# Weight parts moved to other byte offsets inside their tiles

## The chip, the cores and the metric

The kernel runs on one core of one Trainium2 chip. The metric is the device time in microseconds (us); for one core it is the time of that core. Times are medians of several executions; the profile is one further execution.

## The reference, cut to what matters

A decoder of two layers, for 512 tokens of width 1024, in float32. Layer 0 mixes tokens with a gated delta rule (6 heads, run in chunks), layer 1 with sliding-window attention (12 query heads that share two heads of keys and values); both also attend to 256 memory tokens. Each layer ends in a SwiGLU feed-forward of width 2816.

```python
for layer in range(DEPTH):
    h = rms_norm(x, ln_mix[layer])
    mkv = mem_n @ w_mem_kv[layer]
    ...
    x = x + jnp.concatenate([mix_out, mem_o], axis=-1) @ w_out[layer]
    x = x + swiglu(rms_norm(x, ln_ffn[layer]), w_gate_up[layer], w_down[layer])
return rms_norm(x, ln_final)
```

The change touches no product; it concerns where the weights of these products lie in on-chip memory while TensorE reads them.

## The kernel before, in words

**Three products for one.** Every float32 operand of a large product is split into a high part, rounded to the type float32r, and a low part, the remainder. `split` does that with two instructions: ScalarE copies the source to the high part (line 148, by way of `copy`) and VectorE subtracts the high part from the source (line 161, by way of `tt`). `mm3` then issues three matmuls for each 128 rows of the contraction: high weight with high activation, high weight with low activation, low weight with high activation. In the profile the weight tiles are called `whi` and `wlo`, and all these matmuls stand on line 154.

**Two operands, two streams.** In each matmul the weight block of 128x128 floats is the stationary operand: LDWEIGHTS reads 128 floats (512 bytes) from each partition. The activation is the moving operand: 512 floats (2048 bytes) or 256 floats (1024 bytes) are read from each partition while the matmul runs. The load for the next matmul runs beside the present matmul. The profile shows matmuls as engine PE and weight loads as engine PEld.

**Two kinds of weights.** `weight` loads a whole row of weights ([128, 1024], sometimes 768 or fewer columns) from memory, takes a pair of tiles from `parts()` and splits into them. These are the wide weights. They serve `project` (input projections, gates of the feed-forward, queries, output projection), the down projections and the memory keys and values; the moving operand there is nearly always 512 wide. The other kind is narrow. In the feed-forward, two columns of the gate or up matrix are computed at a time by a scheme with seven products of half size in place of eight (`quarters`). Each product takes a weight part of 512 columns and moving operands 256 wide. Those parts lie in a ring of six places: `ring()` takes three pairs of tiles from `parts()` and puts two halves in each pair, and `product` takes the places in turn. A product is four calls of `mm3`, so 12 matmuls; a call of `quarters` has seven products.

**Where the tiles begin.** A weight tile from `parts()` has 1024 + SPARE floats, with SPARE = 64; that is 4352 bytes, 17 times 256. The activation tiles have 2048 bytes and the token sums (tag `T`) 4096. As the program places them, all of these begin at the same place modulo 256 bytes. Every step inside a tile is a multiple of 256 bytes too: 512 bytes from one weight block to the next, 1024 from one half of the tokens to the other, 2048 from one ring half to the other. So the distance modulo 256 between a matmul's moving operand and its weight block is given by the offset inside the weight tile alone. This text calls the distance (moving address minus weight address, modulo 256) the lag. The ring halves begin SHIFT = 16 floats, 64 bytes, into their tile, so their lag is 192. The wide weights begin at offset 0, so their lag is 0. The last down projection takes its weights from another pool (`own`, tag `T`), also with lag 0.

**Order of the work.** Each engine's queue is filled in program order. The stages are: memory keys and values; the delta-rule layer; its output projection; its feed-forward; the attention layer; its output projection; its feed-forward. A feed-forward handles 12 and then 10 of the 22 column pairs; each part is a stretch of ring products followed by a stretch of down projections.

Of the kernel before, what the change touches and what calls it, by code (L numbers as in the profile page):

```python
# [19 lines left out]
T = 512  # L20
# [7 lines left out]
FT = DFF // P  # L28
EPS = 1e-6
LINE = 64  # L30
SHIFT, SPARE = 16, 64
NEG = -1e30
BASE = 32
NB = P // BASE
# [54 lines left out]
class Builder:  # L89
    def __init__(self, tc, a):  # L90
        self.tc, self.nc, self.a = tc, tc.nc, a
        self.n = 0
        self.table, self.table_ins, self.table_users = None, None, []


    def t(self, pool, shape, dtype=F32, tag=None, bufs=None, name=None):
# [96 lines left out]
    def weight(self, src, eng=None, raw=None, parts=1, pool=None, tags=("whi", "wlo"), bufs=3):  # L193

        raw = self.load(src) if raw is None else raw
        n = raw.shape[1]
        if pool is None:
            hi, lo = (x[:, :n] for x in self.parts())
        else:
            hi, lo = (self.t(pool, [P, D], F32R, t, bufs)[:, :n] for t in tags)  # L200
        for i in range(parts):
            s = slice(i * n // parts, (i + 1) * n // parts)
            self.split(raw[:, s], hi[:, s], lo[:, s], eng or self.weng)
        return hi, lo
# [636 lines left out]
    def ffn(self, fp, xp, layer, h, apool, rope=False):  # L841
# [3 lines left out]
        acts, sums, open_pairs, places = [], [], [], []  # L845
# [18 lines left out]
        def ring():  # L864

            if not places:
                for _ in range(3):
                    two = self.parts()
                    places.extend(tuple(x[:, SHIFT + i * T:SHIFT + (i + 1) * T] for x in two) for i in range(2))
            places.append(places.pop(0))  # L870
            return places[-1]

        def begin(f, up, by, tag, bufs, then):

            o = [self.t(fp, [P, T], F32, tag, bufs) for _ in range(2)]
            steps = self.quarters(fp, [col(f + i, up) for i in range(2)], sums, by, o, ring)
            next(steps)
            end()
            next(steps)
            open_pairs.append((steps, then, o))  # L880
            return o
# [13 lines left out]
        for f0, half in ((0, 12), (12, 10)):  # L895
# [16 lines left out]
            for m in range(tail):  # L912
                ps = self.bank("pj")
                for j in (0, 6):
                    n = min(6, half - j)
# [8 lines left out]
        if tail < KD:  # L924
# [9 lines left out]
            for t in parts:  # L934
                acc = self.acc[:, t]
                for m in range(tail, KD):
# [3 lines left out]
                    x = self.x[m][:, t]  # L940
# [295 lines left out]
```

## Time and profile before

| | us |
|---|---|
| Median of 3 runs | 1162.48 (1160.89 to 1162.56) |
| The profiled execution, its own time | 1162.59 |
| Its span, first to last instruction | 1160.8 |
| PE busy | 1135.7 |
| PEld busy | 995.0 |
| DVE (VectorE) busy | 843.1 |
| ACT (ScalarE) busy | 635.5 |

The profiled execution spent 1.79 us outside its span and is 0.11 us above the median, so differences read from the span can be laid on the median as they are. The mean granted TensorE clock is 0.998 of full speed. A matmul's duration in the profile is longer than the time it holds up the next one, since matmuls are pipelined; the pace of a stretch of matmuls is its length divided by their number.

### The profile page before, as it was taken

The numbers are of one execution on the slowest core, as the hardware profiler recorded it, in microseconds if no ns is written. First come the engines' busy times: TensorE is split into PE (matmuls) and PEld (weight loads), VectorE is DVE, ScalarE is ACT, GpSimd is POOL, SyncE is SP. The second block draws the span as 40 slices with busy tenths as digits, with TensorE's granted clock in tenths as the row PEclk, the third lists the DMA queues.
The fourth block names the chain that finished last, engine by engine and source line by source line (L and its number), as shares of the span: only waits on it lengthen the run. The fifth ranks groups of instructions, "written<-read, shape, count | busy, mean of one in ns | idle before, by whom it ended". The sixth has DMA issues, their size and how long they took to land.

```text
span 1160.8 us, 19674 instructions
## 1 busy us (share of the span) xinstructions
PE 1135.7 (98%) x7476; PEld 995.0 (86%) x7476; DVE 843.1 (73%) x1587; ACT 635.5 (55%) x1273; POOL 85.8 (7%) x97
## 2 busy tenths in 40 slices
PE   7999999999999999999999999999999999999996
PEld 6878777877899998899998777677899988999986
DVE  5754877767789987489866767758799843798754
ACT  7569563366556652256653547675566622566533
POOL 0210000000111100011100000010011100111000
PEclk9999999999999999999999999999999999999999
DMA  8433352225567744567723421143477743577232
GB/s 308 129 108 114 115 127 92 73 91 164 163 141 186 188 124 129 151 149 188 173 75 98 136 73 38 55 99 120 113 186 191 175 111 104 150 188 179 74 93 94
DMA packets 73971, 152.83 MB, mean 132 GB/s; under 512 B 17756, under 2 KB 18420, under 8 KB 73876
## 3 DMA queue, kind: packets, MB, share of 16 engines
q1 hardware_dynamic: 62356, 130.59, 35.9%
q0 software_dynamic: 11520, 20.98, 11.5%
q8 instruction: 59, 0.97, 0.4%
q14 instruction: 36, 0.29, 0.1%
HBM read 144.58 MB, written 6.96 MB: 131 GB/s over the span
## 4 chain that ended last, share of the span: by engine, by line
PE 86%; DVE 8%; ACT 2%; DMA 2%; issue 1%; SPq 0%; DVEq 0%; ACTq 0%
PE pj L154 40%; PE g L154 38%; PE sc L154 6%; DVE wlo L161 2%; PE pt L158 1%; DMA wraw<-in_wout 1%; PE g L158 1%; ACT sm L142 1%; DVE l L164 1%; ACT whi L148 1%; DMA wraw<-in_wmk 1%; DVE btmp L161 1%; DVE big L161 0%; DVE sm L752 0%; PE qk L154 0%
## 5 line engine op out<-in xcount | busy, mean ns | idle before, releaser
L148 ACT ACTIVATE whi<-wraw 128x512 fp32r<-128x512 f32 (+2 forms) x331 | 244.2, 745 | 271.9 <-PE pj L154 175.2
L161 DVE TENSOR_TENSOR wlo<-wraw,whi 128x512 fp32r<-128x512 f32 (+2 forms) x331 | 274.3, 838 | 108.6 <-ACT whi L148 102.7
L154 PE MATMUL pj<-h,whi 128*128 128x512 f32 (+1 forms) x676 | 266.4, 395 | 0.8 <-ACT h L148 0.5
L154 PE MATMUL pj<-l,whi 128*128 128x512 f32 (+1 forms) x676 | 265.2, 392 | 1.2 <-DVE l L164 1.2
L154 PE MATMUL pj<-h,wlo 128*128 128x512 f32 (+1 forms) x676 | 265.3, 393 | 0.0
L154 PE MATMUL g<-T,whi 128*128 128x256 f32 x1280 | 230.3, 282 | 0.0
L154 PEld LDWEIGHTS g<-T,whi 128*128 128x128 f32 x1280 | 197.6, 190 | 1.6 <-DVE fu L164 1.6
L154 PE MATMUL g<-T,wlo 128*128 128x256 f32 x640 | 180.1, 281 | 0.0
L154 PEld LDWEIGHTS pj<-h,whi 128*128 128x128 f32 x676 | 127.1, 188 | 29.7 <-issue 3.0
L154 PEld LDWEIGHTS pj<-l,whi 128*128 128x128 f32 x676 | 127.2, 188 | 28.4 <-DVE l L164 2.0
L154 PEld LDWEIGHTS pj<-h,wlo 128*128 128x128 f32 x676 | 127.3, 188 | 26.3 <-issue 1.9
L154 PE MATMUL g<-h,wlo 128*128 128x256 f32 (+1 forms) x508 | 146.2, 288 | 0.0
L154 PE MATMUL g<-l,whi 128*128 128x256 f32 (+1 forms) x508 | 146.1, 288 | 0.0
L154 PE MATMUL g<-h,whi 128*128 128x256 f32 (+1 forms) x508 | 146.0, 287 | 0.0
L154 PEld LDWEIGHTS g<-T,wlo 128*128 128x128 f32 x640 | 120.2, 188 | 0.0
L154 PEld LDWEIGHTS g<-l,whi 128*128 128x128 f32 x508 | 97.5, 192 | 1.2
L154 PEld LDWEIGHTS g<-h,whi 128*128 128x128 f32 x508 | 95.4, 188 | 1.2
L154 PEld LDWEIGHTS g<-h,wlo 128*128 128x128 f32 x508 | 95.4, 188 | 1.2 <-issue 0.2
L985 POOL DMA_DIRECT2D ws<-in_wgu x40 | 35.2, 879 | 722.9 <-ACT sq L151 246.2
L148 ACT ACTIVATE whi<-ws 128x512 fp32r<-128x512 f32 x80 | 50.4, 631 | 51.2 <-PE g L154 42.0
L161 DVE TENSOR_TENSOR fu<-pj,rstd 128x512 f32<-128x512 f32 (+1 forms) x34 | 22.4, 659 | 54.8 <-PE pj L154 54.8
L161 DVE TENSOR_TENSOR wlo<-ws,whi 128x512 fp32r<-128x512 f32 x80 | 54.8, 685 | 6.9 <-ACT whi L148 6.8
(345 smaller groups left out, 1633.0 us busy)
## 6 DMA issues: line engine op xcount, KB each, us to landing
wraw<-in_wgu SPq DMA_DIRECT2D x48, 512.0 KB, 4.1
ws<-in_wgu SPq DMA_DIRECT2D x80, 256.0 KB, 3.5
ws<-in_wgu POOLq DMA_DIRECT2D x80, 256.0 KB, 4.8
wraw<-in_wdn SPq DMA_DIRECT2D x48, 384.0 KB, 3.2
wraw<-in_win SPq DMA_DIRECT2D x26, 512.0 KB, 3.7
wraw<-in_wgu SPq DMA_DIRECT2D x40, 256.0 KB, 4.4
wraw<-in_wout SPq DMA_DIRECT2D x16, 512.0 KB, 3.6
wraw<-in_wdn SPq DMA_DIRECT2D x16, 256.0 KB, 2.7
```

The costliest lines, as they stand in the source:

```text
L142: ins = self.nc.scalar.activation(out, in_, func, **kw).ins
L148: self.copied = self.nc.scalar.activation(out, in_, AF.Copy, **kw).ins
L154: return self.nc.tensor.matmul(out, lhsT, rhs, start=start, stop=stop, skip_group_check=more).ins
L158: return self.nc.tensor.transpose(out, in_, self.ident[:k, :k]).ins
L161: return eng.tensor_tensor(out=out, in0=a, in1=b, op=op).ins
L164: self.nc.vector.scalar_tensor_tensor(out=out, in0=in0, scalar=scalar, in1=in1, op0=op0, op1=op1)
L985: nc.gpsimd.dma_start(s1, a22, accum_op=ALU.add)
```

## The change

The single constant SHIFT goes. Each of the six ring halves gets its own offset, and the wide weights go through four offsets in turn, one step for each call of `weight` without a pool. The tile size stays, since SPARE stays at 64. High and low part of one weight always have the same offset. The numbers of instructions, transfers and waits do not change.

```diff
-SHIFT, SPARE = 16, 64
+NARROW, WIDE, SPARE = ((12, 20), (28, 52), (17, 60)), (4, 8, 60, 62), 64
...
+        self.wide = 0
...
         if pool is None:
-            hi, lo = (x[:, :n] for x in self.parts())
+            o = WIDE[self.wide % len(WIDE)]
+            self.wide += 1
+            hi, lo = (x[:, o:o + n] for x in self.parts())
...
-                for _ in range(3):
+                for shifts in NARROW:
                     two = self.parts()
-                    places.extend(tuple(x[:, SHIFT + i * T:SHIFT + (i + 1) * T] for x in two) for i in range(2))
+                    places.extend(tuple(x[:, o + i * T:o + (i + 1) * T] for x in two) for i, o in enumerate(shifts))
```

In bytes, the ring offsets 12, 20, 28, 52, 17 and 60 are 48, 80, 112, 208, 68 and 240; the lags are 208, 176, 144, 48, 188 and 16. The wide offsets 4, 8, 60 and 62 are 16, 32, 240 and 248 bytes; the lags are 240, 224, 16 and 8. Lag 188 (a ring half) and lag 8 (a quarter of the wide weights) are not multiples of 16; all others are.

## The prediction

> **What bounds the kernel now.** I read the page first, for the engine that is always at work and for the chain that ended last.
>
> ```profile
> span 1160.8 us, 19674 instructions
> PE 1135.7 (98%) x7476; PEld 995.0 (86%) x7476; DVE 843.1 (73%) x1587; ACT 635.5 (55%) x1273; POOL 85.8 (7%) x97
> PEclk9999999999999999999999999999999999999999
> PE 86%; DVE 8%; ACT 2%; DMA 2%; issue 1%; SPq 0%; DVEq 0%; ACTq 0%
> PE pj L154 40%; PE g L154 38%; PE sc L154 6%; DVE wlo L161 2%; PE pt L158 1%; DMA wraw<-in_wout 1%; PE g L158 1%; ACT sm L142 1%; DVE l L164 1%; ACT whi L148 1%; DMA wraw<-in_wmk 1%; DVE btmp L161 1%; DVE big L161 0%; DVE sm L752 0%; PE qk L154 0%
> ```
>
> TensorE sets the end: matmuls of line 154 into the banks `pj` and `g` make up 40% and 38% of the chain, and the granted clock is full in every slice. So the question is the pace of matmuls, and whether that pace depends on the lag. The page's mean durations cannot answer it, because matmuls overlap. The long unbroken pieces of the chain of waits can: start, length, and the number of matmuls in it.
>
> ```profile
> 97.65 1.78 PE g L154 x16
> 182.38 1.78 PE g L154 x16
> ...
> 301.73 16.32 PE pj L154 x72
> 335.27 97.52 PE g L154 x828
> 435.53 64.17 PE pj L154 x283
> 499.70 97.52 PE g L154 x828
> 830.96 97.52 PE g L154 x828
> 995.42 97.52 PE g L154 x828
> 1144.97 5.88 PE pj L154 x49
> ```
>
> The first pieces of these stages already separate three cases.
> - Wide weights, 512 moving, lag 0: 16.32 us / 72 = 226.7 ns a matmul; the down projections give 64.17 / 283 = 226.7 as well.
> - Ring, 256 moving, lag 192: 97.52 / 828 = 117.8 ns, the same in all four feed-forward parts.
> - The last piece, two down projections with 256 moving and lag 0: 5.88 / 49 = 120.0 ns.
>
> Two things follow. First, at lag 0 going from 256 to 512 columns adds 226.7 - 120.0 = 106.7 ns. A matmul has one weight load beside it at either width, so 106.7 ns is the price of 256 columns beside which no weights are loaded. The 256 columns with a load beside them cost 120.0 at lag 0 and 117.8 at lag 192. So the load costs the stream 13.3 ns at lag 0 and 11.1 ns at lag 192, and 2.2 ns of that goes with the only address difference between the two cases that the code shows. Second, a lower end: a 256-wide matmul cannot be expected under 106.7 ns, nor a 512-wide one under 213.4.
>
> **The change part by part.** The counts come from the groups by form.
>
> ```profile
> L154 PE MATMUL g<-T,whi 128*128 128x256 f32 x1280 | 230.3, 282 | 0.0
> L154 PE MATMUL g<-T,wlo 128*128 128x256 f32 x640 | 180.1, 281 | 0.0
> L154 PE MATMUL g<-h,wlo 128*128 128x256 f32 x480 | 135.1, 282 | 0.0
> L154 PE MATMUL g<-l,whi 128*128 128x256 f32 x480 | 135.1, 281 | 0.0
> L154 PE MATMUL g<-h,whi 128*128 128x256 f32 x480 | 135.1, 281 | 0.0
> ```
>
> The ring has 1280 + 640 + 3 x 480 = 3360 matmuls, 560 for each half, every one of them at the pace above and on the chain. One nanosecond on the ring's mean pace is 3.4 us. For the wide weights I take what lies on the chain: 40% of the span in `pj` at 226.7 ns is 0.40 x 1160.8 / 0.2267 = 2048 matmuls, some 512 for each of the four offsets. One nanosecond there is 2.0 us. The matmuls outside the chain wait for something else and gain or lose nothing.
>
> The new lags are in no trace, only 192 and 0 are. I interpolate between these two points, linearly around the circle of 256 bytes: 64 bytes from lag 192 to lag 0 for 2.2 ns, so 0.035 ns a byte, and no more than 2.2 ns beyond lag 0.
>
> The ring, distance from 192 and price: lag 208, 16 bytes, 0.55 ns; lag 176, 16 bytes on the other side, 0.55; lag 188, 4 bytes, 0.14; lag 144, 48 bytes, 1.66; lags 48 and 16 are farther than lag 0, 2.2 each. The mean is (0.55 + 0.55 + 0.14 + 1.66 + 2.2 + 2.2) / 6 = 1.2 ns, and 1.2 x 3360 = **+4.1 us**. From both sides: 0 if none of the lags is worse than 192, +7.4 us if all are like lag 0 (2.2 x 3360). A gain is not excluded, since nothing shows that 192 is the best lag: 11.1 ns of cost are still there.
>
> The wide weights, by the same line: lag 240 lies 16 bytes from lag 0 on the way to 192, -0.55 ns; lag 224, 32 bytes, -1.1; lags 16 and 8 lie on the side away from 192, nothing. The mean is -0.41 ns, and -0.41 x 2048 = **-0.8 us**. From both sides: -4.5 us if every lag but 0 is as good as 192 (2.2 x 2048); upward, one half of the load cost again (half of 13.3) on the one lag that starts inside a 16-byte unit, 6.7 x 512 = +3.4 us.
>
> The splits write the parts, so they change too. In the ring the two engines that split have room:
>
> ```profile
> core 0: us, PE busy (x) PEld busy (x) DVE busy (x) ACT busy (x) POOL busy (x), PEclk, DMA share, GB/s
> 335.00:433.00 98.00, 98.00 (x832) 97.92 (x831) 86.91 (x156) 61.62 (x118) 12.94 (x15) 1.00 0.68 169
> 435.50:499.70 64.20, 64.20 (x286) 53.18 (x285) 37.19 (x56) 16.09 (x22) 4.37 (x5) 1.00 0.46 130
> ```
>
> VectorE works 86.91 of 98 us in a ring stretch, 11.1 us of room. Of its splits of ring parts there (ten calls of `quarters` with seven products, 70), one in six, about 12, would get the offset of 68 bytes; each would have to take 0.9 us longer before VectorE became late. Whether an odd offset costs VectorE anything at all, the convolution of the delta-rule layer shows: it reads and writes its tile 4, 8 and 12 bytes past the start.
>
> ```profile
> L164 DVE SCALAR_TENSOR_TENSOR qv<-pj,gains,qv x36: 731/742/750, 143.0 to 251.7; 128x511 f32<-128x511 f32 x12, 128x510 f32<-128x510 f32 x12, 128x509 f32<-128x509 f32 x12
> L164 DVE SCALAR_TENSOR_TENSOR l<-x,gains,h x32: 739/746/752, 285.1 to 812.1; 128x512 fp32r<-128x512 f32 x32
> ```
>
> The median is 742 ns at odd offsets and 746 ns at even ones, so I cost the splits at nothing; ScalarE, which has more room, I cost at nothing by analogy. If that cover went, all 12 splits of a stretch would cost at most what exceeds 11.1 us.
>
> The sum: +4.1 - 0.8 = +3.3 us on the span, 1164.1; on the profiled execution 1165.9; on the median, 1162.48 + 3.3 = 1165.8 us.
>
> A rule of the Trainium skill speaks against any effect. "SBUF — State Buffer", section Who interferes with whom, gives TensorE two independent read ports, one for the moving operand and one for LDWEIGHTS, and says that it waits for nobody. By it the two streams cannot disturb each other and the sum would be zero; the trace's 120.0 against 117.8 ns does not agree, though it does not show which resource they share.
>
> **The rivals.**
>
> *The wide weights gain and the ring keeps its pace (faster).* Perhaps lag 0 is a singular bad case: both reads start on the same unit of 256 bytes, and any other start avoids that. For it: the moving stream reads 1024 bytes while the load reads 512, so it moves past the load through the whole circle of 256 bytes twice, whatever the starting distance; most lags should then be alike, and only a lag near 0, where such a passing falls on the start and the end, should differ. Two pieces above fit too: the sixteen matmuls at 97.65 (key with key, lag 0) and at 182.38 (query with key, lag 192) both take 1.78 us, 111 ns each. These are plain 128-wide float32 products, where both operands have the same width, and the lag does nothing there. Against it: lags 8 and 16 are close to 0. Price: -2.2 x 2048 = -4.5 us for the wide weights, and the half with lag 16 may lose up to 2.2 x 560 = 1.2 us: between 1158.0 and 1159.2.
>
> *Nothing depends on the lag (same).* The 2.2 ns may come from something else in which the two cases differ: the seven-product scheme against plain accumulation, other tiles, other work of VectorE beside it. For it: the rule on the ports above, and the two equal pieces of 1.78 us. Against it: the ring reads the same kind of weight tiles, split by the same two instructions, as the last down projections. Time: 1162.5.
>
> *Starts inside a 16-byte unit cost a second read (slower, more).* The half with lag 188 begins 4 bytes past a multiple of 16, the quarter with lag 8 begins 8 bytes past one. If such a load has to fetch each group of four floats in two steps, the cost of the load to the stream could double: +11.1 ns on 560 matmuls and +13.3 ns on 512, that is 6.2 + 6.8 = 13 us on top of +3.3: 1178.8. It decides as soon as the extra cost on these two exceeds about 2 ns a matmul. Against it: the convolution's rows, though those are another engine. The same page of the Trainium skill, section Specifications (TRN2), gives SBUF lines of 16 bytes with a penalty for each crossing to a new line; 512 bytes from such a start touch 33 lines and not 32, which would be far less than a doubling, and no trace here shows TensorE reading from such a start.
>
> **How the numbers follow.** The forecast, lags priced by their distance, gets 0.44; the gain of the wide weights 0.26; nothing 0.18; the costly starts 0.12. Two times of this kernel can be told apart from about 0.2%, 2.3 us. The forecast lies 3.3 us up, so some 0.07 of its 0.44 falls inside that bound; of the gain nearly all lies outside. Faster 0.26, same 0.25, slower 0.49. The forecast's own range is 1162.5 to 1170 (ring 0 to +7.4). The range reaches down to the gain of the wide weights, 1158.0, less a further 0.5 for a ring that improves a little, and upward to lag 0's price on the whole ring plus the half-priced bound on the wide weights, 1162.5 + 7.4 + 3.4 = 1173.3: 1157.5 to 1173.3. Left outside are the full doubling and deeper gains.
>
> **What would show it right or wrong.** The pieces of the chain in the ring should be longer: 97.52 us for 828 matmuls becomes 98.5 at a mean pace of 119.0. Single ring halves should differ in steps of 12 matmuls, lags 48 and 16 near 120 ns, lags 208, 176 and 188 near 118. The down projections should stay near 226.3, with every fourth weight or so at 225.6. It is wrong if the ring keeps 117.8 while the wide pieces fall to 224.5, if both paces stay as they are, or if the half with lag 188 stands out above 122 ns. A longer time with both paces unchanged would mean that the splits, and not the reads, cost it; then the chain would show more of `wlo` line 161 than 2%.

## The result, and the profile after

The changed kernel takes 1171.41 us (four runs, 1171.05 to 1171.76); the kernel before took 1162.52 in the same session. The ratio is 1.0081, 95% interval 1.0068 to 1.0095: slower by 8.9 us.

The page after, in the lines that answer to those of before:

```profile
span 1169.6 us, 19674 instructions
PE 1146.8 (98%) x7476; PEld 997.3 (85%) x7476; DVE 843.8 (72%) x1587; ACT 636.5 (54%) x1273; POOL 85.9 (7%) x97
PEclk9999999999999999999999999999999999999999
PE pj L155 44%; PE g L155 39%; PE sc L155 6%; DVE wlo L162 1%; PE pt L159 1%; PE g L159 1%; ACT sm L143 1%; DMA wraw<-in_wmk 1%; DVE l L165 0%; DVE sm L755 0%; ACT whi L149 0%; DVE btmp L162 0%; PE qk L155 0%; DVE q L162 0%; DVE big L162 0%
```

Same instructions, same clock; VectorE and ScalarE are busy as before within a microsecond, PE 11 us longer. The chain has more of `pj`, the wide weights. Its long pieces (start, length, matmuls) give the paces:

```profile
302.53 16.68 PE pj L155 x72
336.86 98.21 PE g L155 x828
437.82 65.69 PE pj L155 x283
503.52 98.21 PE g L155 x828
836.18 98.21 PE g L155 x828
1002.79 98.21 PE g L155 x828
1153.81 5.85 PE pj L155 x49
```

The ring went from 97.52 to 98.21 us for 828 matmuls, 117.8 to 118.6 ns each. The down projections went from 64.17 to 65.69 for 283, 226.7 to 232.1 ns. The last piece, with 256 moving columns and 30 of its 49 weights from the pool that was not touched, hardly moved.

The trace gives the starts of successive matmuls, so the pace can be sorted by lag: here the distance from the moving operand of the running matmul to the weight block that is loaded beside it, which is the next matmul's. These are means over the trace ("by starts" below), with intervals that hold a stall left out (over 150 ns for the ring, over 260 ns for the wide weights):

| | lag: ns from start to start |
|---|---|
| ring, before | 192: 117.7 |
| ring, after | 208: 118.3; 188: 118.5; 176: 118.6; 144: 119.8; 48: 116.9; 16: 119.6 |
| wide, before | 0: 227.4 |
| wide, after | 240: 232.9; 224: 233.0; 16: 228.6; 8: 233.2 |

Three of the four wide lags cost nearly 6 ns, the fourth 1.2; the ring's six average 0.9 ns more than 192.

These paces make more than 8.9 us: some 2300 wide intervals at 4.5 ns are 10.4 us, the ring's four pieces 4 x 0.69 = 2.8, and the other 256-wide matmuls give back about 0.3: 12.9 us. The rest is in stalls. Gaps of over 600 ns between two matmuls sum to 18.3 us before and 14.4 us after, 3.9 less, and 12.9 - 3.9 = 9.0, close to the 8.9 measured. Of the 3.9 us, 3.0 lie ahead of matmuls on wide weights, most of them in the second output projection. The waits between 770 and 820 us, before and then after (who waited for whom: sum in us, times, longest):

```profile
ACT whi L148 <- DMA wraw<-in_wout: 6.8, 2, 5.3
```
```profile
ACT whi L149 <- DMA wraw<-in_wout: 4.5, 2, 2.8
```

The slowest transfer of weights in that window took 8.0 us to land before and 5.4 us after. The same wait was 6.6 us in the first experiment below and 4.4 us in the second. In the run below that moves only the last wide weight ahead of each ring stretch, and keeps every other weight where it was before, it was 4.5 us. So it varies without the change, and I don't count it as the change's doing.

### The profile page after: what moved, and what is told of

It is laid out like the page before. It is cut to its first block, busy times and chain, and to the rows that moved or that the text cites. A ratio compares the mean times of both kernels' runs of the same rounds, so it can differ in the third digit from the quotient of the medians.

```text
span 1169.6 us, 19674 instructions
## 1 busy us (share of the span) xinstructions
PE 1146.8 (98%) x7476; PEld 997.3 (85%) x7476; DVE 843.8 (72%) x1587; ACT 636.5 (54%) x1273; POOL 85.9 (7%) x97
## 4 chain that ended last, share of the span: by engine, by line
PE 90%; DVE 5%; ACT 2%; issue 1%; DMA 1%; SPq 0%; DVEq 0%; ACTq 0%
PE pj L155 44%; PE g L155 39%; PE sc L155 6%; DVE wlo L162 1%; PE pt L159 1%; PE g L159 1%; ACT sm L143 1%; DMA wraw<-in_wmk 1%; DVE l L165 0%; DVE sm L755 0%; ACT whi L149 0%; DVE btmp L162 0%; PE qk L155 0%; DVE q L162 0%; DVE big L162 0%
```

## The experiments

All are compared with runs of the kernel before on the same chip; that took 1160.35, 1160.84 and 1160.58 us in the three sessions below. Ring offsets of 16 floats and wide offsets of 0 mean "as in the kernel before".

**The wide offsets alone.**

```diff
-NARROW, WIDE, SPARE = ((12, 20), (28, 52), (17, 60)), (4, 8, 60, 62), 64
+NARROW, WIDE, SPARE = ((16, 16), (16, 16), (16, 16)), (4, 8, 60, 62), 64
```

> The ring goes back to 16 floats in every half (lag 192), the wide weights keep their four new offsets. In the changed kernel a ring stretch of 828 matmuls takes 98.21 us against 97.52, four times 0.69, so the ring's part of the loss of 8.9 us should be 2.8 us. If the two parts simply add, this kernel takes 1171.4 - 2.8 = 1168.6 us, with ring pieces of 97.52 us and down pieces of 65.7 us for 283. Rival (the splits cost the time and not TensorE's reads): the paces need not come apart by kind of weight; the ring's pieces may stay at 98.2.

It took 1155.33 us, ratio 0.9953 (0.9938 to 0.9968): faster than the kernel before by 5.0 us, where 1168.6 was expected. The chain's pieces:

```profile
302.46 16.68 PE pj L155 x72
336.79 93.86 PE g L155 x828
433.45 65.69 PE pj L155 x283
828.64 93.85 PE g L155 x828
```

The wide weights cost what they cost in the changed kernel. But the ring, at exactly the addresses and the lag of the kernel before, runs at 93.86 / 828 = 113.4 ns and not at 117.8. Over 3360 matmuls that is 14.8 us won against about 10 lost. So a pace is not a function of the lag alone.

**The ring offsets alone.**

```diff
+NARROW, WIDE, SPARE = ((12, 20), (28, 52), (17, 60)), (0,), 64
```

> The six ring offsets are new, the wide weights are back at offset 0. If the parts add: 1162.5 + 2.8 = 1165.3 us, ring pieces of 98.2 us, down pieces of 64.17 us for 283. Rival (the splits): down pieces stay near 65.7.

1162.97 us, ratio 1.0027 (1.0015 to 1.0039), 2.6 us slower; the theory said 2.8.

```profile
334.48 98.23 PE g L155 x828
435.47 64.17 PE pj L155 x283
```

The ring pays its part (98.23 us against 98.21 in the changed kernel), the wide pieces are those of before. The splits (the rival) are out: the paces come apart by kind of weight, and in the changed kernel's ring stretch VectorE is busy 86.82 of 98 us, against 86.91 before.

```profile
336.86:434.86 98.00, 98.00 (x828) 98.00 (x828) 86.82 (x156) 61.19 (x117) 12.93 (x15) 1.00 0.68 167
```

**The activations moved, no weight part moved.**

```diff
+NARROW, WIDE, SPARE = ((16, 16), (16, 16), (16, 16)), (0,), 64
...
+                    pool("pad").tile([P, 56], F32, name="pad")
                     self.bpool, xp = pool("actb"), pool("x")
```

> The kernel before with every weight offset as it was (ring 16 floats, wide 0), and 224 unused bytes ahead of one pool of activations (actb). So the activations in that pool begin 224 bytes further, and no weight part has moved. Matmuls of wide weights with these activations then have lag 224, as a quarter of the wide weights has in the changed kernel: the gates of the first feed-forward, the output projection of the second layer, the first eight of the contraction blocks in the second feed-forward's down projections. All others keep lag 0. Theory (the distance between the two reads sets the pace): 512-wide matmuls with lag 224 take 233 ns; the gates of the first feed-forward go from 16.32 to 16.8 us for 72, those of the second stay at 16.37; the first feed-forward's down piece stays at 64.17 us, the second's goes to about 65.5 us. 672 matmuls at +5.7 ns give +3.8 us: 1166.3, the ring's h matmuls of the first feed-forward (lag 160) aside. Rival (the weight block's own address sets the pace): no weight has moved, so all wide pieces stay at 226.7 ns a matmul, and the time at 1162.5.

1164.34 us, ratio 1.0031 (1.0018 to 1.0043), 4.0 us slower; the theory said 3.8. The pieces of this run: the last three of the first feed-forward's four gates, its down projections, then the same of the second.

```profile
319.18 16.79 PE pj L155 x72
435.94 64.17 PE pj L155 x283
814.59 16.34 PE pj L155 x72
931.20 65.59 PE pj L155 x283
```

The two whose activations lie in the moved pool (the second down projections with eight of their twelve blocks) go to 233.2 and 231.8 ns, the other two stay at 226.7 and 226.9. The weights lie where they lay, so it is the distance between the two reads that counts, and not the weights' own place: the rival is out.

The same trace also shows one lag at two paces inside one stretch. In the first feed-forward's ring, matmuls with `h` and `l` now have lag 160, those with `T` still lag 192, and the two kinds take turns. By starts, a group of 12 matmuls at lag 192 that follows 24 at lag 160 settles at 113.3 ns; a group of 36 at lag 192 that follows 12 at lag 160 runs at 117.8, and this repeats through both stretches.

**One lag for each stretch, two kernels.**

```diff
+NARROW, DOWN, WIDE, SPARE = (48, 56, 40, 32), (16, 32, 48, 56), 0, 64
...
+                    two, o = self.parts(), NARROW[2 * layer + (f0 > 0)]
...
+            self.wide = DOWN[2 * layer + (f0 > 0)]
```

> One lag for each stretch. The ring of the four feed-forward parts has offsets 48, 56, 40 and 32 floats: lags 64, 32, 96, 128. The four stretches of down projections have offsets 16, 32, 48 and 56 floats: lags 192, 128, 64, 32. All other wide weights are at offset 0. Theory of the prediction (price grows with the distance from lag 192, 2.2 ns at 64 bytes and no more): ring pieces of 828 at 120 ns, 99.4 us, for lags 64, 32 and 96, and 99.4 for 128; down piece of lag 192 at 224.5 ns, 63.5 us for 283, the others at 226.7. Rival (each width has a curve of its own, as the changed kernel's 117 ns for ring lag 48 and 233 ns for wide lags 224, 240 and 8 suggest): ring at lags 64 and 32 near 117, down projections between 225.5 and 233, and the same lag need not be good for both.

> One lag for each stretch, as in the first scan. Ring offsets 0, 54, 50 and 4 floats: lags 0, 40, 56, 240. Down projections at offsets 60, 63, 1 and 24 floats: lags 16, 4, 252, 160. Theory (each width has its own curve, offset inside a 16-byte unit is nothing by itself): lag 0 in the ring 120 ns, 40 and 56 between 116.7 and 117.8; down at lag 16 as in the changed kernel, 228.6 ns; lags 4 and 252, which start 4 bytes beside lag 0, between 227 and 233. Rival (a start inside a 16-byte unit costs a second read): lags 4 and 252 clearly above 233, 240 ns or more.

The second kernel has (0, 54, 50, 4) and (60, 63, 1, 24). One run each, 1169.12 and 1170.29 us. Of the first, the four ring pieces (lags 64, 32, 96, 128; in the second, 811 matmuls were recorded) and two down pieces (lags 192, 64):

```profile
334.94 97.52 PE g L155 x828
435.25 66.03 PE pj L155 x283
501.28 94.57 PE g L155 x811
832.10 99.35 PE g L155 x828
934.24 64.79 PE pj L155 x283
999.03 99.36 PE g L155 x828
```

Of the second, ring lags 0 and 240, and down lags 16 and 252:

```profile
334.38 99.35 PE g L155 x828
436.50 64.63 PE pj L155 x283
935.55 65.76 PE pj L155 x283
1001.32 97.98 PE g L155 x828
```

The linear price of the prediction fell. In the ring 64 costs the same as 192 (117.8 ns), 32 is better (116.6), and 0, 40, 56, 96 and 128 all give 120.0. For wide weights 192 is not the better lag but a bad one: 66.03 / 283 = 233.3 ns, where 224.5 was expected. The best of these is 0, then 16 and 64 (228.4 and 228.9). A lag has two prices, one for each width. Offsets inside a 16-byte unit cost nothing by themselves: by starts, the wide lags 4 and 252 take 233.3 and 232.4 ns, like the aligned 192 and 32, which take 233.3.

**Only the last wide weight ahead of each ring stretch moved.** The ring at 16 floats, all wide weights at 0 but the last ahead of each ring stretch:

```diff
+            o = LAST if self.last else WIDE[self.wide % len(WIDE)]
...
+                self.last = len(whole) == 3
                 whole.append(gate(len(whole)))
...
+                    self.last = (f0, m, j) == (0, KD - 1, 6)
                     w = down(m, j, n)
```

> The kernel before (ring 16 floats, wide 0) but for one thing: the last wide weight ahead of each of the four ring stretches (the fourth gate, or the last down weight; 24 or 18 matmuls) has offset 4, lag 240. In the run with the new wide offsets alone the ring, whose addresses are those of the kernel before, ran at 113.4 ns and not 117.8. Theory (the two reads have more than one lasting pace at the same lag, and the matmuls just ahead of a stretch decide which it falls into): all four ring pieces at 113.3 ns, 93.9 us for 828; down pieces unchanged at 64.17; the time falls by 4 x 3.66 = 14.6 us, less 84 matmuls at +6 ns: 1160.35 - 14.1 = 1146.2 us. Rival (something that the wide offsets did over the whole program, such as the time at which splits run beside the ring): one weight ahead of each stretch does nothing, ring pieces 97.52 us, time 1160.9.

1161.76 us, ratio 1.0005 (0.9996 to 1.0015): nothing, and the rival's time. All four ring pieces are 97.52 us. The moved weight ahead of the first stretch, and that stretch:

```profile
331.11 5.44 PE pj L155 x24
336.55 97.52 PE g L155 x828
```

5.44 / 24 = 226.7 ns at lag 240, where lag 240 took 232.9 in the changed kernel. The same lag again has two paces.

**All wide weights moved but that last one.** The same code with `WIDE = (4, 8, 60, 62)` and `LAST = 0`.

> The opposite: the ring at 16 floats, all wide weights at their new four offsets, except the last one ahead of each ring stretch, which is back at offset 0. Theory (the matmuls just ahead decide): ring back at 117.8 ns, 97.52 us for 828; wide pieces as in the changed kernel, 65.7 us for 283; so 1155.3 + 14.6 = 1169.9 us. Rival (the wide offsets over the whole program): ring stays at 113.4, time 1155.3.

1168.72 us, ratio 1.0070 (1.0053 to 1.0086), the theory's side: 84 matmuls put back to lag 0 take the ring from 113.4 ns back to 117.8, at unchanged wide paces elsewhere.

```profile
337.57 97.52 PE g L155 x828
437.82 65.60 PE pj L155 x283
```

So what comes just ahead of a ring stretch at lag 192 decides the pace of the 828 matmuls behind it, and the wide offsets as such do not.

**Other ring lags behind a moved last weight.**

> As the run with the last wide weight alone moved (lag 240 ahead of each ring stretch, all other wide weights at lag 0), with another ring lag in each stretch: 48, 64, 32, 208. Theory (pace depends on lag and on what came just ahead): some of these also fall to 113.3 ns; lags 64 and 32 had 117.8 and 116.7 after other forerunners. Rival (113.3 belongs to lag 192 alone): 116.9, 117.8, 116.7 and 118.4 as before.

One run, 1160.6 us. Ring lags 48, 64, 32, 208:

```profile
334.41 96.60 PE g L155 x828
497.99 97.52 PE g L155 x828
829.37 96.60 PE g L155 x828
992.93 97.98 PE g L155 x828
```

116.7, 117.8, 116.7 and 118.3 ns: the rival's numbers. Lag 240 ahead turns nothing, as in the run that moved the last weight alone.

**Lag 224 or lag 8 on the last weight.** `LAST = 8`, and `LAST = 62`.

> As the run with only the last wide weight ahead of each ring stretch moved, but to offset 8 (lag 224) and not 4 (lag 240); there the moved weight itself stayed at 226.7 ns, and the ring at 117.8. Theory (there are two lasting phases between the two reads: one in which a wide matmul takes 227 ns and the ring's 117.8, one in which they take 233 and 113.3; lag 240 only keeps the phase it meets, while 224 or 8 turn it): the moved weights run at about 233 ns, the ring pieces at 113.3 ns, 93.9 us for 828, and the time falls by 14.6 us less 84 x 6 ns = 0.5: 1160.8 - 14.1 = 1146.7 us. Rival (only a mix of lags over the whole program brings the ring's faster pace): ring pieces 97.5 us, time 1161.

> The same with offset 62 (lag 8) for the last wide weight ahead of each ring stretch. Theory (two phases, lag 8 turns it): as with lag 224, ring 113.3 ns, about 1146.7 us. Rival: 117.8 and 1161.

With lag 224: 1162.35 us, ratio 1.0018 (1.0009 to 1.0027). The moved weights do turn to 233 ns, but the ring stays at 97.52 us: this half of the theory fell.

```profile
329.43 5.83 PE pj L155 x25
335.26 97.52 PE g L155 x828
```

With lag 8: 1147.21 us, ratio 0.9889 (0.9876 to 0.9903), 13.4 us faster than the kernel before and some 24 us under the changed one. The last moved weight and the ring behind it:

```profile
329.92 5.60 PE pj L155 x24
335.52 4.55 PE g L155 x40
```

The chain's long pieces (three of the four ring stretches; in one, 780 matmuls were recorded):

```profile
335.52 93.85 PE g L155 x828
432.19 64.30 PE pj L155 x283
496.49 88.43 PE g L155 x780
822.34 93.86 PE g L155 x828
918.98 64.30 PE pj L155 x283
```

24 matmuls at 233.3 ns, then 113.4 ns in the ring, and the wide weights are back at their cheap pace as soon as lag 0 returns. The gain is the ring's: 3360 x 4.4 = 14.8 us, less 84 x 6 ns = 0.5, makes 14.3, of which the time shows 13.4.

**The scan behind lag 224.**

> The last wide weight ahead of each ring stretch at lag 224, and ring lags 176, 208, 48, 64 in the four stretches. Theory (two phases): lags near 192 may hold the faster phase too, 113 to 115 ns; lag 64, which ran at 117.8 like lag 192 in the other phase, should go to 113.3. Rival (the phase matters at lag 192 alone): 118.5, 118.3, 116.8, 117.8 as met before.

One run, 1162.56 us; lags 176, 208, 48 and 64 gave 118.8, 117.8, 116.7 and 117.8 ns by starts. None fell to 113, and lag 224 did not turn the ring at lag 192 either. But lag 208 took 118.3 ns behind lag 240 (the last piece of the earlier scan) and takes 117.8 here, so lag 192 is not the only one with two paces in the ring; with one run of each, what chose between them is not shown:

```profile
500.32 97.52 PE g L155 x828
```

**All wide weights at lag 240.**

```diff
+NARROW, WIDE, SPARE = ((16, 16), (16, 16), (16, 16)), (4,), 64
```

> All wide weights at offset 4 (lag 240), the ring at 16 floats throughout. Theory (lag 240 keeps the phase it meets, it is lags 224 and 8 that turn it): wide matmuls at 226.7 ns, 64.2 us for 283, ring at 117.8, time 1161. Rival (lag 240 itself costs 6 ns a matmul, as its mean of 232.9 ns in the changed kernel reads): down pieces 65.8 us, and the time 1161 + 12 if the ring stays at 117.8, or 1158 if it falls to 113.3.

1157.12 us, ratio 0.9975 (0.9966 to 0.9984). The wide weights run at 66.03 / 283 = 233.3 ns, the ring behind them at 113.3:

```profile
337.10 93.84 PE g L155 x828
433.75 66.03 PE pj L155 x283
```

The theory was wrong here, the rival's second case (1158) right: reached from the start of the program, lag 240 has the dear pace; reached from a stretch at lag 0, the cheap one. Lag 240 is thus seen at 226.7 and at 233.3 ns, and the ring's 192 at 117.8 and at 113.3.

## Why the prediction was right and wrong, point by point

**What bounds the kernel: right.** TensorE's pace beside the weight loads moved the time, and it depends on the distance between the two reads: the run with moved activations shows that it is the distance and not either address alone.

**The ring's term: the size about right, the curve wrong.** Predicted +4.1 us, measured +2.8 by the pieces and 2.6 by the run with the ring alone. But the price does not grow with the distance from 192: the farthest, 48, is the cheapest (116.9 against a predicted 120.0), and 188, close by, costs 0.7 ns where 0.14 was predicted. Two points do not make a curve on a circle of 256 bytes.

**The wide term: the sign wrong.** Predicted -0.8 us, measured about +10 by the paces. The failing step is the transfer of the ring's comparison, lag 192 better than lag 0, to matmuls of twice the width. Lag 192 costs wide weights 233.3 ns; no lag was met that beats the 226.7 of lag 0. The upper bound given to this term, +3.4 us for a single lag, was too low for the same reason: three lags of four cost 6 ns each. That a load costs the stream the same at either width was assumed at lag 0, to get the 106.7 ns, and then taken for a rule at every lag. At lag 192 it fails: the ring's 117.8 and the wide 233.3 differ by 115.5 ns (by 120.0 at the ring's other pace), and not by 106.7.

**The stalls: not in the sum.** 3.9 us came back in shorter waits, most of it at transfers of the output projection. Without them the result, at about 1175.3, would have left the range at its upper end (1173.3).

**The time: luck.** The forecast said slower by 3.3 us, and it is slower by 8.9, above the forecast's own range (1162.5 to 1170) and inside the full range only because shorter waits, which no term held, hid nearly a third of the loss. The direction came from the ring's term, which turned out the smaller part of the loss; the larger part, the wide weights, was forecast as a gain.

**The rivals.** *The wide weights gain*: wrong in its mechanism. At none of the other lags did the wide weights gain; they lost at all of them, save for the 84 matmuls at lag 240 right behind lag 0, which stayed at 226.7 ns. That a change of the wide offsets alone can be faster is true, but by the ring behind them. *Nothing depends on the lag*: out. The rule of the Trainium skill that it rested on ("SBUF — State Buffer", section Who interferes with whom: two independent read ports, TensorE waits for nobody) does not agree with the run that moved only the activations and took 233 in place of 227 ns. *Starts inside a 16-byte unit*: out; the half with lag 188 took 118.5 ns, between its neighbours 176 and 208, and wide lags 4 and 252 are no dearer than aligned ones.

**What the prediction took for granted and no step named:** that a lag has one price. The 2.2 ns between lags 0 and 192 at 256 columns, through which its whole line is drawn, are 120.0 less 117.8; with the ring's other pace it would have been 120.0 less 113.3, three times as much. Because one lag has several paces, the parts do not add: the ring alone costs 2.6 us, the wide offsets alone win 5.0, and both together lose 8.9. The changed kernel pays for the dear wide pace without the ring at lag 192 that could have used what it leaves behind.

**What stays open.** What carries the pace from one matmul to the next is not shown, nor why lag 8 ahead of the ring turns it and lag 224 alone does not. In the run with the wide offsets alone the first two ring stretches are reached from a weight at lag 224 as well, and run at 113.4; there that weight follows others at lag 240, 8 and 16, in the run with the last weight alone at lag 224 it follows lag 0.

## What to carry to other kernels

When one engine's pace is the bound, read that pace from unbroken pieces of the chain (length over count) and not from mean durations: half a nanosecond on 3360 matmuls is seen there, or in the starts, and not in the durations of matmuls that overlap. Where weights are read beside a running matmul, the distance between the two reads is a parameter worth a scan, with one value for each long stretch, for each width by itself, and with what comes ahead of the stretch kept fixed. Test parts of such a change alone: here the sum of the parts has the other sign from the whole, and the best version moves 84 matmuls.

## What the runs showed of the hardware that was not expected

**More than one lasting pace at one distance.** At the same addresses, the ring runs at 117.8 or at 113.3 ns for a whole stretch of 828 matmuls, whichever it fell into in its first few; a wide weight at lag 240 runs at 226.7 or 233.3. A pace lasts while the lag stays: in the run with moved activations it is settled anew at each return to lag 192.

**The costs seem to come in steps.** This is an estimate, for it takes the load to cost the same at both widths at lag 0, which no run tests by itself. Then 256 columns without a load beside them cost 226.7 - 120.0 = 106.7 ns. Over that, the load costs 6.6 ns at the fast ring pace (113.3), 13.3 at 120.0 and 226.7 - 213.4, and 19.9 at 233.3: about one, two and three times 6.7 ns. Many lags lie between these, at means that repeat over a few matmuls, and the wide lag 160, at 234.2 by starts, lies a little above.

**A cheap stretch can pay for a dear forerunner.** The lasting pace that is dear for 512 columns (233) goes with the cheap one for 256 (113) in all three runs where the ring kept 113 for whole stretches, though not the other way: lag 224 on the last weight gave 233 and left the ring at 117.8.
